# Convolution tiles moved to later heads of a recurrence, and two compressions moved behind the projections around them, in a three-block network on one core

## The chip, the core and the metric

The kernel runs on one core of a Trainium2 chip. The metric is the device time of one execution in microseconds, shown as the median of several runs. TensorE (PE) multiplies matrices, VectorE (DVE) and ScalarE (ACT) do the elementwise work, GpSimd (POOL) has little to do here, and SyncE (SP) issues the loads and stores.

## What is computed

Three blocks run one after the other on 512 tokens of width 1024. The change touches the second and the third.

The second block has an attention branch with compressed keys and values. Of its reference this matters:

```
q, kc, vc, ks, vs, kw, vw, z, gl = jnp.split(h @ w_in_b, ...)
def compress(t, pos, w1, w2):
    blocks = heads_kv(t)[:, :, cmp_idx] + pos
    flat = blocks.reshape(Bsz, N_KV, n_cmp, L_CMP * HEAD_DIM_2)
    return jax.nn.silu(flat @ w1) @ w2
k_cmp = compress(kc, pos_ck, w_ck1, w_ck2)
v_cmp = compress(vc, pos_cv, w_cv1, w_cv2)
...
g = jax.nn.sigmoid(gb)
return g[..., 0:1] * o_cmp + g[..., 1:2] * o_slc + g[..., 2:3] * o_win
```

The third block runs a gated recurrence of eight heads of width 128 in both directions, in chunks of 128 tokens, and beside it a convolution of 31 taps over 1024 channels, which is normalised over the channels:

```
o_lat, _, _ = hgrn2_bidir(pq, pi, pff, pfb, lbs[0, l], lbs[1, l], s_f, s_b)
o = rmsnorm_3(o_hg, gn_w) * silu(heads(g));   y_hg = o.reshape(...) @ w_hg_out
u = cv_a * sigmoid(cv_b)
u = silu(layernorm_3(dwconv1d(u, dw_w, dw_b), ln_w, ln_b));   y_cv = u @ w_cv_out
y = sigmoid(gate_hg) * y_hg + sigmoid(gate_cv) * y_cv
```

The normalisation needs all 1024 channels of the convolution before its first value exists.

## The kernel before

**Products.** A weight tile of 128 x 1024 is loaded (`wr`), split by ScalarE into a rounded part `wh` (L127) and by VectorE into a remainder `wl` (L128), and TensorE multiplies each of the eight pieces three times (L141 to L143). One such product of 24 matmuls is called a form here; it gives 128 output columns for all 512 tokens. Three PSUM buffers hold the forms, so a form can start when the one three before it has been read. The products with 256 columns have lines L182 to L184.

**Order.** The code is written stage by stage, and a scheduler orders the instructions of each engine ahead of time by priority and readiness. Each engine then runs its list strictly in that order and waits where an operand is late.

**Second block.** `blocks` copies the key and value products into strided blocks (L753 on VectorE, L755 on ScalarE). `compress` multiplies them with a loaded matrix (16 matmuls, L765), takes column 124 as a bias (L767), applies SiLU on ScalarE (L770), multiplies again (L775 for keys, L785 for values) and copies the result out (L779, L787). `values(0)` and `values(1)` are forms whose results VectorE copies (L793). The gate logits are one form of 48 columns, copied by ScalarE, transposed by TensorE and passed through Tanh.

**Third block.** The recurrence handles head after head. `gla_gates` makes the decays of two heads (L1009, L1019, L1020), `gla_front` the running sums of a head (L1118 to L1126), and `gla_back` the rest: exponentials and products on six levels (L1144 to L1161, with matmuls L1151 and L1167), masks (L1173 to L1179), the key transposes (L1201), state products (L1206) and the state chain on VectorE (L1209), the output products (L1213 to L1215), the squares (L1219), a reciprocal root in ten small VectorE steps (L225 to L234), the scaling (L1221, one for each head), a transpose (L1226) and the gate (L1227), and the split into `yhgh` and `yhgl` (L132, L133). `gla_back` is emitted at a higher priority.

Beside head j the code emits the pieces that the string `BESIDE[j]` names. `cN` is convolution tile N: two forms, then on VectorE L1260, L1262 and 30 taps L1264 that each update the tile `cy` in place, a store to DRAM, and, some pieces later, the statistics over its transpose (L260 on TensorE, L262 on VectorE). `gN` and `hN` are each one form of gate logits with a Tanh and a store. The string sets the order of emission; the order on the engines is the scheduler's.

After the last head the statistics are closed (L269, the reciprocal root again, and four transposes L253 each for mean and root). Eight forms with `w_hg_out` read all heads (evacuated by L1314); while they run, each channel tile of the convolution is loaded back, reduced by the mean (L1318), scaled (L1319), put through SiLU on ScalarE (L1320) and split (L132, L133, into `ycvh` and `ycvl`). Eight forms with `w_cv_out` then read all of those (evacuated by L1326).

Of the kernel before, what the change touches and what calls it, by code (L numbers as in the profile page):

```python
# [693 lines left out]
def branch_a(k, hT):  # L694

    nc, I = k.nc, k.I
    cw, cb = k.col("conv_w", (P, 8, 3)), k.col("conv_b", (P, 8))
    nc.vector.tensor_scalar(cw, cw, 0.5, None, op0=ALU.mult)
    nc.vector.tensor_scalar(cb, cb, 0.5, None, op0=ALU.mult)
    y = k.b16(F32R, name="yAh"), k.b16(F32R, name="yAl")  # L700
    m = []
    yield y, m
    for j in range(8):
        cg = k.f("cg")
        nc.scalar.activation(cg, k.form_a(I["w_a2"][8 + j], hT), AF.Copy)
        u = k.f("cu", (P, S + 2))
        nc.gpsimd.memset(u[:, :2], 0.0)
        nc.vector.tensor_mul(u[:, 2:], cg, k.form_a(I["w_a2"][16 + j], hT))
        c = k.f("cc")
        nc.vector.tensor_scalar(c, u[:, :S], cw[:, j, 0:1], cb[:, j:j + 1], op0=ALU.mult, op1=ALU.add)  # L710
        nc.vector.scalar_tensor_tensor(c, u[:, 1:S + 1], cw[:, j, 1:2], c, op0=ALU.mult, op1=ALU.add)
        nc.vector.scalar_tensor_tensor(c, u[:, 2:], cw[:, j, 2:3], c, op0=ALU.mult, op1=ALU.add)
        nc.vector.tensor_mul(c, c, k.form_a(I["w_a2"][j], hT))
        z = k.f("cz")
        k.silu2(z, k.form_a(I["w_a2"][24 + j], hT))
        nc.gpsimd.tensor_mul(c, c, z)
        k.split(y[0][:, j], y[1][:, j], c)
        yield
    m.append(k.b16(name="mT"))
    for j in range(8):  # L720
        branch(k, 0, y, hT, m[0], (j,))
        yield


def block2(k, ctx, hT, x2d, x3d):
# [4 lines left out]
    c4 = k.wk.tile([P, 4, P], F32, name="c4", tag="c4", bufs=1)  # L730
# [9 lines left out]
    def blocks(nm):  # L740
        kg = k.b16(shape=(P, 16, 125), name="kg")
        nc.sync.dma_start(out=kg[:, :, 124], in_=I["pos_c" + nm])
        for tl in range(2):
            ps = first.pop(0) if first else k.form_a(I["w_c" + nm][tl], hT)
            for hf in range(2):
                hh = 2 * tl + hf
                v = ps[64 * hf:64 * hf + 64].rearrange("p (j m b) -> p b m j", m=8, b=2)
                for b in range(2):
                    for mh in range(2):
                        o = kg[64 * b:64 * b + 64, 8 * mh:8 * mh + 8, 31 * hh:31 * hh + 31]  # L750
                        i_ = v[:, b, :, mh:mh + 31]
                        if mh:
                            nc.vector.tensor_copy(o, i_)  # L753
                        else:
                            nc.scalar.activation(o, i_, AF.Copy)  # L755
        return kg

    def compress(nm, kg):
        ph = k.mm((P, 125))
        for q in range(2):  # L760
            w1 = k.x4("w1", (P, 8, P))
            nc.sync.dma_start(out=w1, in_=I[f"w_c{nm}1"][:, 8 * q:8 * q + 8])
            for m in range(8):
                mm_i = 8 * q + m
                nc.tensor.matmul(ph, lhsT=w1[:, m], rhs=kg[:, mm_i], start=mm_i == 0, stop=mm_i == 15)  # L765
        pb = k.small((P, 1), "pb", bufs=2)
        nc.vector.tensor_copy(pb, ph[:, 124:125])  # L767
        hs = k.wk.tile([P, 4, 32], F32, name="hs", tag="B", bufs=3)
        nc.vector.memset(hs, 0.0)
        nc.scalar.activation(hs[:, :, :31], ph[:, :124].rearrange("p (h j) -> p h j", h=4), AF.Silu, bias=pb)  # L770
        if nm == "k":
            w2 = k.wk.tile([P, P], F32, name="w2", tag="B", bufs=3)
            nc.sync.dma_start(out=w2, in_=I["w_ck2"])
            pk = k.mm((P, P))
            nc.tensor.matmul(pk, lhsT=w2, rhs=hs.rearrange("p a b -> p (a b)"), start=True, stop=True)  # L775
            pk = pk.rearrange("p (a b j) -> p a b j", a=2, b=2)
            for par in range(2):
                rr = slice(64 * par, 64 * par + 64)
                nc.vector.tensor_copy(kcmp[rr, :, par], pk[rr, :, par])  # L779
        else:  # L780
            w2 = k.wk.tile([P, 64], F32, name="w2", tag="B", bufs=3)
            nc.sync.dma_start(out=w2, in_=I["w_cv2"])
            for kp in range(2):
                pv = k.mm((64, 64))
                nc.tensor.matmul(pv, lhsT=hs[:, 2 * kp:2 * kp + 2].rearrange("p a b -> p (a b)"), rhs=w2, start=True, stop=True)  # L785
                for i in range(2):
                    nc.vector.tensor_copy(vbd[32 * i:32 * i + 32, kp, i], pv[32 * i:32 * i + 32])  # L787
# [3 lines left out]
    def values(b):  # L791
        t = k.x4("vs", (P, NT, 256))
        k.form_b(I["w_vs"][b], hT, lambda i, c, ps: nc.vector.tensor_copy(t[:, i:i + c], ps), nat)  # L793
        VV.append(t)
    first = k.forms_a([I["w_ck"][0], I["w_ck"][1], I["w_cv"][0]], hT)
    kg = blocks("k"), blocks("v")
    values(0)
    compress("k", kg[0])
    values(1)
    compress("v", kg[1])  # L800
    ps = k.form_a(I["w_gl"], hT, n=48)
    gt = k.f("gt", (48, S))
    nc.scalar.activation(gt, ps, AF.Copy)
# [4 lines left out]
    gv = gN.rearrange("p n h b -> p n (h b)")  # L808
    nc.scalar.activation(gv, tps, AF.Tanh, scale=0.5)
    nc.vector.tensor_scalar(gv, gv, 0.5, 0.5, op0=ALU.mult, op1=ALU.add)  # L810
    ON = k.b16(shape=(P, NT, 16, 64), name="ON")
    fill = branch_a(k, hT)
    yA, mA = next(fill)
    lo, hi = slice(0, 64), slice(64, P)
    for kp in range(2):
# [12 lines left out]
        for i in range(4):  # L828
# [31 lines left out]
            for n in range(NT):  # L860
                nc.tensor.matmul(po[:, n].rearrange("p a b -> p (a b)"), lhsT=pt[:, n], rhs=vbd[:, kp].rearrange("p a b -> p (a b)"), start=True, stop=True)
            nc.vector.tensor_mul(ON[:, :, hs], po, l[:, :, :, None].to_broadcast([P, NT, 2, 64]))
            for par in range(2):
# [33 lines left out]
                for b in range(2):  # L897
                    nc.gpsimd.tensor_add(ON[:, :, h], ON[:, :, h], ot[:, :, b])
                next(fill, None)
# [5 lines left out]
    for j in range(8):  # L905
# [3 lines left out]
        for n in range(NT):  # L909
            nc.tensor.transpose(tps[:, n], ON[:, n, 2 * j:2 * j + 2].rearrange("p a b -> p (a b)"), k.ident)  # L910
        c = k.f("cc")
# [67 lines left out]
    v = k.small((P, NT), "rs_v")  # L979
# [116 lines left out]
LEVELS = (128, 64, 32, 16, 8)  # L1096
DIAG = 4
BEFORE = "c0 g0 v0 c1 v1 g1 c2 v2 g2 c3 v3 g3"
BESIDE = ("c4 g4", "c5 g5", "h0 g6", "c6 g7", "h1", "c7 h2", "h3 h4", "h5 h6 h7")


def gla_gates(k, h, hT):
# [128 lines left out]
def block3(k, hT, x3d, out):  # L1231
# [44 lines left out]
    def run(items):  # L1276
        for it in items.split():
            n = int(it[1])
            for t in late:
                t[0] -= 1  # L1280
            while late and late[0][0] < 0:
                late.pop(0)[1]()
            {"c": lambda: conv(n), "v": lambda: value(n), "g": lambda: gate("w_gcv", n, gcd), "h": lambda: gate("w_ghg", n, ghd)}[it[0]]()
# [10 lines left out]
    for j in range(-1, 8):  # L1294
# [7 lines left out]
        with k.tc.high_priority(offset=GLA_AHEAD):  # L1302
            gla_back(k, j, hT, V, R[:, j % 2], q[:, j % 2], tot[j], masks, gnw, DB, y)
        run(BESIDE[j])
    for t in late:
# [99 lines left out]
def body(tc, I, out):  # L1405
    with ExitStack() as es:
        k = K(es, tc, I)
        w = k.w(I["w_in_a"][0], KT, offset=FIRST)
        x = load_x(k)
        k.setup()  # L1410
        x2d = k.dr.tile([P, KT, S], F32, name="x2d")
        x3d = k.dr.tile([P, KT, S], F32, name="x3d")
        k.vec_input(0)
        k.add_vec("Bc", "w_mod", "b_mod", 0)
        k.add_vec("Ac", "w_mod", "b_mod", 1, ("norm1_w",), True)
        k.vec_input(1)
        k.add_vec("B2", "w_ada", "b_ada", 0)
        k.add_vec("A2", "w_ada", "b_ada", 1, ("g_pre",), True)
        k.add_vec("G2", "w_ada", "b_ada", 2, ("g_post",))
        k.vec_input(2)  # L1420
        k.add_vec("B3", "w_mod", "b_mod", 0)
        k.add_vec("A3", "w_mod", "b_mod", 1, ("norm1_w",), True)
        k.add_vec("gt1", "w_mod", "b_mod", 2)
        k.add_vec("B4", "w_mod", "b_mod", 3)
        k.add_vec("A4", "w_mod", "b_mod", 4, ("norm2_w",), True)
        k.add_vec("gt2", "w_mod", "b_mod", 5)
        ctx = ctx_steps(k)
        acc, h1 = block1(k, ctx, w, *x)
        h2 = block1b(k, ctx, acc, h1, x2d)
        h3 = block2(k, ctx, h2, x2d, x3d)  # L1430
        block3(k, h3, x3d, out)
# [128 lines left out]
```

## Time and profile before

| what | value |
|---|---|
| median of 3 runs | 3153.04 us (3151.38 to 3154.02) |
| the profiled execution | 3153.95 us, of which the span is 3152.2 us |
| TensorE busy | 3049.8 us, 97% of the span |
| VectorE busy | 2064.1 us, 65% |
| ScalarE busy | 1255.9 us, 40% |

Shares are means over stages that have different limits. In the recurrence VectorE is busy far above its mean, and in most other stages far below.

### The profile page before, as it was taken

The page shows a single profiled execution, that of the slowest core. Times are in us where ns is not written, and L with a number is a line of the kernel's source. Part 1 is how long each engine was busy: PE and PEld are TensorE (multiplying, and loading weights), DVE is VectorE, ACT ScalarE, POOL GpSimd, SP SyncE. Part 2 cuts the span into 40 slices and gives each one's busy share as a digit, 9 for nine tenths or more (in the row PEclk, how much of TensorE's full clock was granted, in tenths as well). Part 3 has the DMA queues.
Part 4 walks back from the last instruction along what each step waited for, and adds up shares of the span by engine and source line. Part 5 has one row for each costly group of instructions (what it writes and reads, how often), then busy time and mean ns, then how long its engine had stood idle before and what let it go on. Part 6 is the DMA issues. An engine that isn't in the chain of part 4 may idle for free.

```text
span 3152.2 us, 45055 instructions
## 1 busy us (share of the span) xinstructions
PE 3049.8 (97%) x17508; PEld 2538.7 (81%) x17508; DVE 2064.1 (65%) x4223; ACT 1255.9 (40%) x2111; POOL 144.9 (5%) x224
## 2 busy tenths in 40 slices
PE   9999999999999999999999999999998989999998
PEld 7888878787887787778778888889877777888886
DVE  7566665656545745555444364589998996597877
ACT  4333544444442533334443233442454544243322
POOL 0000000000000001110110101000000000100000
PEclk9999999999999999999999999999999999999998
DMA  8324343434322421221122222443222225323332
GB/s 292 101 94 134 103 159 137 159 131 151 129 79 68 135 85 65 67 67 61 54 71 93 94 94 88 139 137 107 94 80 72 88 86 170 107 84 94 96 99 77
DMA packets 113062, 334.43 MB, mean 106 GB/s; under 512 B 17616, under 2 KB 23760, under 8 KB 112848
## 3 DMA queue, kind: packets, MB, share of 16 engines
q1 hardware_dynamic: 112848, 331.54, 31.9%
q8 instruction: 138, 2.26, 0.3%
q14 instruction: 76, 0.62, 0.1%
HBM read 316.82 MB, written 14.68 MB: 105 GB/s over the span
## 4 chain that ended last, share of the span: by engine, by line
PE 47%; DVE 5%; ACT 2%; issue 1%; DVEq 0%; ACTq 0%
PE mm L141 13%; PE mm L142 13%; PE mm L143 13%; PE O L891 1%; PE mm L182 1%; PE mm L183 1%; PE mm L184 1%; DVE wl L128 1%; PE S L875 1%; PE T L884 1%; ACT wh L127 0%; PE S L1167 0%; DVE cy L1264 0%; PE S L1206 0%; PE S L942 0%
## 5 line engine op out<-in xcount | busy, mean ns | idle before, releaser
L127 ACT ACTIVATE wh<-wr 128x1024 fp32r<-128x1024 f32 (+2 forms) x499 | 503.2, 1010 | 1084.0 <-PE mm L142 799.6
L128 DVE TENSOR_TENSOR wl<-wr,wh 128x1024 fp32r<-128x1024 f32 (+2 forms) x499 | 605.1, 1214 | 426.2 <-ACT wh L127 422.1
L141 PE MATMUL mm<-h2h,wh 128*128 128x512 f32 (+1 forms) x752 | 300.8, 400 | 7.7 <-DVE kg L753 6.8
L142 PE MATMUL mm<-h2l,wh 128*128 128x512 f32 (+1 forms) x752 | 300.3, 399 | 0.0
L143 PE MATMUL mm<-h2h,wl 128*128 128x512 f32 (+1 forms) x752 | 300.2, 399 | 0.0
L141 PE MATMUL mm<-h3h,wh 128*128 128x512 f32 x488 | 193.8, 403 | 7.7 <-ACT th L1270 4.2
L142 PE MATMUL mm<-h1l,wh 128*128 128x512 f32 x488 | 198.8, 407 | 0.0
L141 PE MATMUL mm<-h1h,wh 128*128 128x512 f32 x488 | 197.5, 405 | 0.0
L143 PE MATMUL mm<-h1h,wl 128*128 128x512 f32 x488 | 197.2, 404 | 0.0
L142 PE MATMUL mm<-h3l,wh 128*128 128x512 f32 x488 | 193.5, 401 | 0.0
L143 PE MATMUL mm<-h3h,wl 128*128 128x512 f32 x488 | 193.2, 401 | 0.0
L1264 DVE SCALAR_TENSOR_TENSOR cy<-uc,dww,cy 128x512 f32<-128x512 f32 x240 | 176.9, 746 | 2.4
L141 PEld LDWEIGHTS mm<-h2h,wh 128*128 128x128 f32 (+1 forms) x752 | 141.7, 188 | 34.2 <-issue 7.2
L142 PEld LDWEIGHTS mm<-h2l,wh 128*128 128x128 f32 (+1 forms) x752 | 141.8, 189 | 25.2
L143 PEld LDWEIGHTS mm<-h2h,wl 128*128 128x128 f32 (+1 forms) x752 | 141.5, 188 | 24.6
L369 DVE CUSTOM_DVE_ANT_0 gr<-gr,crow 128x256 f32<-128x256 f32 x352 | 131.5, 425 | 42.9 <-DMA gr<-in_w_mod 31.4
L141 PE MATMUL mm<-h4h,wh 128*128 128x512 f32 (+1 forms) x368 | 140.5, 382 | 0.0
L143 PE MATMUL mm<-h4h,wl 128*128 128x512 f32 (+1 forms) x368 | 140.5, 382 | 0.0
L142 PE MATMUL mm<-h4l,wh 128*128 128x512 f32 (+1 forms) x368 | 140.5, 382 | 0.0
L1369 DVE SCALAR_TENSOR_TENSOR fc<-up,fdw,fc 128x512 f32<-128x512 f32 x176 | 132.2, 751 | 5.1
L881 ACT ACTIVATE pe<-sb,nm 128x128 f32<-128x128 f32 (+3 forms) x128 | 71.4, 558 | 119.4 <-DVE nm L878 119.2
L141 PEld LDWEIGHTS mm<-h3h,wh 128*128 128x128 f32 x488 | 93.2, 191 | 27.8 <-ACT th L1270 4.7
(532 smaller groups left out, 7238.5 us busy)
## 6 DMA issues: line engine op xcount, KB each, us to landing
gr<-in_w_mod SPq DMA_DIRECT2D x64, 512.0 KB, 5.1
wr<-in_w_up SPq DMA_DIRECT2D x44, 512.0 KB, 3.5
wr<-in_w_in_a SPq DMA_DIRECT2D x32, 512.0 KB, 3.5
wr<-in_w_f SPq DMA_DIRECT2D x32, 512.0 KB, 3.5
wr<-in_w_v SPq DMA_DIRECT2D x32, 512.0 KB, 3.8
wr<-in_w_in_b SPq DMA_DIRECT2D x32, 512.0 KB, 3.5
wr<-in_w_a SPq DMA_DIRECT2D x32, 512.0 KB, 3.5
gr<-in_w_ada SPq DMA_DIRECT2D x24, 512.0 KB, 4.5
```

The lines of the kernel that those rows point to most:

```text
L127: self.nc.scalar.activation(h, r, AF.Copy)
L128: self.nc.vector.tensor_sub(l, r, h.bitcast(F32))
L141: mm(ps, lhsT=wh[:, k], rhs=xh[:, k0 + k, tok], start=first and k == 0, stop=False)
L142: mm(ps, lhsT=wh[:, k], rhs=xl[:, k0 + k, tok], start=False, stop=False)
L143: mm(ps, lhsT=wl[:, k], rhs=xh[:, k0 + k, tok], start=False, stop=last and k == kt - 1)
L182: mm(ps, lhsT=sel(xh, k), rhs=wh[:, kk], start=st, stop=False)
L183: mm(ps, lhsT=sel(xh, k), rhs=wl[:, kk], start=False, stop=False)
L184: mm(ps, lhsT=sel(xl, k), rhs=wh[:, kk], start=False, stop=en)
L369: nc.vector.tensor_tensor_reduce(out=r[:, sl], in0=r[:, sl], in1=self.crow[:, sl], scale=1.0, scalar=0.0, op0=ALU.mult, op1=ALU.add, accum ...
L881: nc.scalar.activation(pe, sb, AF.Exp, bias=m, scale=-1.0, accum_out=lt[:, n, b:b + 1])
L1264: nc.vector.scalar_tensor_tensor(c, u[:, t:t + S], dww[:, j, t:t + 1], c, op0=ALU.mult, op1=ALU.add)
L1369: nc.vector.scalar_tensor_tensor(c, u[:, a:a + 8, b:b + 64], fw[:, j, t:t + 1], c, op0=ALU.mult, op1=ALU.add)
```

## The change

Two independent pieces of order are edited. In the second block both compressions are emitted after the second `values` and after the gate logits; before, one compression stood behind each `values`. In the third block the string `BESIDE` deals the last four convolution tiles and the gates to the heads in another order: tiles 4, 5, 6 and 7 stood beside heads 0, 1, 3 and 5 and now stand beside heads 0, 3, 6 and 7. No instruction is added to or taken from the work itself.

```diff
     first = k.forms_a([I["w_ck"][0], I["w_ck"][1], I["w_cv"][0]], hT)
     kg = blocks("k"), blocks("v")
     values(0)
-    compress("k", kg[0])
     values(1)
-    compress("v", kg[1])
     ps = k.form_a(I["w_gl"], hT, n=48)
     gt = k.f("gt", (48, S))
     nc.scalar.activation(gt, ps, AF.Copy)
@@
     nc.scalar.activation(gv, tps, AF.Tanh, scale=0.5)
     nc.vector.tensor_scalar(gv, gv, 0.5, 0.5, op0=ALU.mult, op1=ALU.add)
+    compress("k", kg[0])
+    compress("v", kg[1])
     ON = k.b16(shape=(P, NT, 16, 64), name="ON")
@@
-BESIDE = ("c4 g4", "c5 g5", "h0 g6", "c6 g7", "h1", "c7 h2", "h3 h4", "h5 h6 h7")
+BESIDE = ("c4 h0 g4", "h1 g5", "h2", "c5 h3 g6", "h4 g7", "h5", "c6 h6", "h7 c7")
```

**First place: TensorE at the compressions.** Before, the key compression stands between the two `values` products (L182 to L184, from which two rows are shown on either side):

```order
L183 MATMUL mm<-wl,h2h 128x256
L184 MATMUL mm<-wh,h2l 128x256
L765 MATMUL mm<-kg,w_9609 128x125 x8
L765 MATMUL mm<-kg,w_9619 128x125 x8
L775 MATMUL mm<-hs,w_9634 128x128
L182 MATMUL mm<-wh,h2h 128x256
L183 MATMUL mm<-wl,h2h 128x256
```

Of the changed kernel, from the last matmuls of the gate logits on:

```order
L142 MATMUL mm<-h2l,wh 48x512
L143 MATMUL mm<-h2h,wl 48x512
L765 MATMUL mm<-kg,w_9763 128x125 x7
L804 MATMUL T<-ident,gt 128x48 x4
L765 MATMUL mm<-kg,w_9763 128x125
L765 MATMUL mm<-kg,w_9773 128x125 x8
L775 MATMUL mm<-hs,w_9788 128x128
L765 MATMUL mm<-kg,w_9795 128x125 x8
L765 MATMUL mm<-kg,w_9805 128x125 x8
L785 MATMUL mm<-w_9820,hs 64x64 x2
```

Both compressions now stand in one piece behind the gate logits, whose transposes (L804) have moved in among the key compression's matmuls; the key and the value compression have only each other to cover their waits.

**Second place: VectorE in the middle of the recurrence, at the mask steps and the state chain of head 2** (L1177, L1179 and L1209; the taps of a convolution tile are L1264). Before, at the second mask step:

```order
L1177 COPY_PREDICATED D<-masks,S 128x128
L1264 SCALAR_TENSOR_TENSOR cy<-uc,dww,cy 128x512
L128 TENSOR_TENSOR wl<-wr,wh 128x1024
L1264 SCALAR_TENSOR_TENSOR cy<-uc,dww,cy 128x512
L1179 COPY_PREDICATED A<-masks,D 128x512
L1264 SCALAR_TENSOR_TENSOR cy<-uc,dww,cy 128x512
L262 BN_STATS bst<-T 128x6
```

The same steps of the changed kernel:

```order
L1177 COPY_PREDICATED D<-masks,S 128x128
L1209 SCALAR_TENSOR_TENSOR SS<-SS,dec,S 128x128
L1179 COPY_PREDICATED A<-masks,D 128x512
L1209 SCALAR_TENSOR_TENSOR SS<-SS,dec,S 128x128 x2
L1118 SCALAR_TENSOR_TENSOR R_18837<-rst,sp 128x512
```

Before, a tap stood behind nearly every step of head 2, its state chain included; now the masks and the state chain follow one another and no tap stands there.

**Third place: VectorE behind the last head.** Before, the closing root (L223 is its last step) stands ahead of the first evacuation of a `w_hg_out` form (L1314):

```order
L223 SCALAR_TENSOR_TENSOR rs_y<-rs_t,rs_y 128x4
L128 TENSOR_TENSOR wl<-wr,wh 128x1024
L233 TENSOR_TENSOR rs_a<-rs_y 128x4
L234 TENSOR_TENSOR rs_a<-rs_a,rs_c 128x4
L223 SCALAR_TENSOR_TENSOR rs_y<-rs_a,rs_y 128x4
L1314 SCALAR_TENSOR_TENSOR yT<-th,mm 128x512
L1318 TENSOR_TENSOR cy<-cy,S 128x512
```

Of the changed kernel, from the seventh of the eight evacuations on:

```order
L1314 SCALAR_TENSOR_TENSOR yT<-th,mm 128x512
L128 TENSOR_TENSOR wl<-wr,wh 128x1024
L1264 SCALAR_TENSOR_TENSOR cy<-uc,dww,cy 128x512 x6
L128 TENSOR_TENSOR wl<-wr,wh 128x1024
L262 BN_STATS bst<-T 128x6 x2
L269 BN_AGGR mv_22772<-bst 128x2 x2
```

The taps of tile 7 and the closing statistics now stand beside the `w_hg_out` forms, and the normalisation (L1318, L1319) stands behind the last of the eight evacuations; before, it stood among them.

## Rows read from the trace of the kernel before

**Rows 1.** The page, part 1: busy time and share of each engine.
```profile
PE 3049.8 (97%) x17508; PEld 2538.7 (81%) x17508; DVE 2064.1 (65%) x4223; ACT 1255.9 (40%) x2111; POOL 144.9 (5%) x224
```

**Rows 2.** The waits of PE over the run: total us, times, longest.
```profile
PE mm L301 <- DVE ss L294: 13.2, 4, 5.3
PE O L1215 <- DVE SS L1209: 9.9, 2, 7.4
PE mm L141 <- DVE kg L753: 6.8, 1, 6.8
...
PE S L1151 <- DVE rs_y L226: 4.6, 1, 4.6
```

**Rows 3.** Windows between the eight L1221: busy us and instructions, clock, DMA.
```profile
core 0: us, PE busy (x) PEld busy (x) DVE busy (x) ACT busy (x) POOL busy (x), PEclk, DMA share, GB/s
...
2289.05:2354.03 64.98, 57.85 (x533) 46.16 (x531) 63.76 (x111) 33.54 (x45) 0.16 (x2) 0.95 0.26 86
2354.03:2400.74 46.71, 37.06 (x290) 29.57 (x289) 44.71 (x88) 18.56 (x42) 0.16 (x2) 0.89 0.18 63
2400.74:2452.83 52.09, 50.61 (x510) 40.48 (x508) 44.53 (x82) 31.98 (x42) 0.00 (x0) 1.00 0.22 74
2452.83:2506.58 53.75, 51.18 (x431) 41.17 (x427) 53.01 (x95) 22.85 (x40) 0.16 (x2) 1.00 0.26 87
2506.58:2545.63 39.05, 38.72 (x432) 30.50 (x424) 38.27 (x74) 29.39 (x46) 0.00 (x0) 1.00 0.24 74
2545.63:2595.04 49.41, 44.69 (x303) 36.00 (x298) 48.05 (x85) 20.64 (x38) 0.00 (x0) 0.97 0.29 92
2595.04:2622.32 27.28, 19.84 (x291) 16.66 (x292) 21.23 (x54) 14.12 (x31) 3.85 (x6) 0.75 0.15 48
2622.32:2672.60 50.28, 50.07 (x229) 41.20 (x228) 34.55 (x61) 22.16 (x28) 0.00 (x0) 1.00 0.72 226
```

**Rows 4.** Windows, a stretch of the first block that holds only forms.
```profile
100.00:150.00 50.00, 50.00 (x222) 41.44 (x221) 20.69 (x24) 13.61 (x17) 0.23 (x2) 1.00 0.34 113
```

**Rows 5.** VectorE's groups by form, 2289 to 2622 us: first and last of 41.
```profile
L1264 DVE SCALAR_TENSOR_TENSOR cy<-uc,dww,cy 128x512 f32<-128x512 f32 x116 | 86.3, 744 | 0.0
L128 DVE TENSOR_TENSOR wl<-wr,wh 128x1024 fp32r<-128x1024 f32 x41 | 50.1, 1221 | 4.0 <-ACT wh L127 3.5
...
L1119 DVE MEMSET R<- 128x1 f32 x5 | 0.3, 59 | 0.0
```

**Rows 6.** VectorE's timeline: start us, us; runs of one line.
```profile
2226.07 3.90 DVE L1264 SCALAR_TENSOR_TENSOR cy<-uc,dww,cy 128x512 f32<-128x512 f32 x5
...
2587.65 1.89 DVE L1158 TENSOR_TENSOR E<-R 128x512 f32<-128x512 f32 x3
```

**Rows 7.** TensorE's timeline at the two compressions.
```profile
1103.49 3.73 PE L765 MATMUL mm<-kg,w 128*128 128x125 f32 x32
1109.51 0.49 PE L775 MATMUL mm<-hs,w 128*128 128x128 f32 x2 [2.28 <-ACT hs L770]
1121.34 3.73 PE L765 MATMUL mm<-kg,w 128*128 128x125 f32 x32
1125.79 0.45 PE L785 MATMUL mm<-w,hs 128*64 128x64 f32 x4 [0.71 <-ACT hs L770]
```

**Rows 8.** ScalarE's timeline there and at the SiLU of the normalisation.
```profile
1107.79 1.28 ACT L770 ACT_TABLE_LOAD   x1 [3.53 <-DVE pb L767]
1109.09 0.36 ACT L770 ACTIVATE hs<-mm,pb 128x124 f32<-128x124 f32 x1
...
1132.72 0.58 ACT L803 ACTIVATE gt<-mm 48x512 f32<-48x512 f32 x1
...
2637.90 1.28 ACT L1320 ACT_TABLE_LOAD   x1 [3.22 <-DVE cy L1319]
2639.20 0.82 ACT L1320 ACTIVATE cy<-cy,clb,clw 128x512 f32<-128x512 f32 x1
2639.92 1.04 ACT L127 ACTIVATE wh<-wr 128x1024 fp32r<-128x1024 f32 x1
2640.87 0.61 ACT L132 ACTIVATE ycvh<-cy 128x512 fp32r<-128x512 f32 x1
```

**Rows 9.** TensorE's timeline after its wait for the block copies L753.
```profile
1084.94 0.76 PE L141 MATMUL mm<-h2h,wh 128*128 128x512 f32 x1 [6.81 <-DVE kg L753]
...
1088.07 0.42 PE L142 MATMUL mm<-h2l,wh 128*128 128x512 f32 x1
```

**Rows 10.** VectorE's timeline behind the last head: the last split and the last evacuation.
```profile
2658.36 0.69 DVE L133 TENSOR_TENSOR ycvl<-cy,ycvh 128x512 fp32r<-128x512 f32 x1
...
2671.93 0.69 DVE L1314 SCALAR_TENSOR_TENSOR yT<-th,mm 128x512 f32<-128x512 f32 x1 [3.35 <-PE mm L143]
```

## The prediction, made before the changed kernel was run

> **What bounds the kernel now.** I read the page first. TensorE is busy for 97% of the span and VectorE for 65% [rows 1], so over the whole run only TensorE's gaps can be won back, about 100 us of them. The list of what TensorE waited for comes next [rows 2]: its largest entries sit in the final stage and at the block copies, which the change does not touch, but the state chain of the recurrence (L1209) holds it for 9.9 us in two waits and another VectorE step for 4.6 us in one. The third view cuts the recurrence at the eight scalings L1221 [rows 3]. I call the piece that ends at head k's scaling stretch k. The reader should compare three columns. In stretches 1, 2, 4 and 6 VectorE is busy for 63.8 of 65.0, 44.7 of 46.7, 53.0 of 53.7 and 48.1 of 49.4 us, so VectorE ends those stretches, and TensorE idles for 7.1, 9.7, 2.6 and 4.7 us in them. In stretches 3 and 5 TensorE is nearly full. In stretch 7 neither is: TensorE works for 19.8 of 27.3 us, because the list ahead of the last scaling has little but the head's own chain. Together the seven take 333.3 us with 33.3 us of TensorE idle. The piece behind head 7, up to the first `w_cv_out` matmul, is TensorE alone: 50.1 of 50.3 us, with VectorE at 34.6.
>
> So this is a stage in which two engines take turns as the bound, and what an edit of the order can win is TensorE's idle time, at most the 33 us, less whatever it opens elsewhere.
>
> **The change part by part: the recurrence.** I counted the form matmuls in TensorE's order per stretch. Before they are 194, 110, 168, 183, 121, 152 and 37; after, 211, 63, 177, 162, 192, 70 and 132. The sum rises from 965 to 1007, because forms that used to follow (a gate, tile 7, and the first 28 matmuls of `w_hg_out`) now run ahead of head 7's scaling. One takes 0.225 us (222 in 50 us, [rows 4]). What a stretch of before takes beyond its forms is 21.3, 22.0, 14.3, 12.6, 11.8, 15.2 and 19.0 us [rows 3]: the head's own small matmuls and the idle time. The four stretches 3 to 6 have a mean of 13.5, with 11.8 and 15.2 as ends.
>
> For VectorE I took every instruction of the order at the mean of its group [rows 5], less 0.08 us, since consecutive ones overlap by that much (three of 0.684 us take 1.89, [rows 6]). For before this gives 63.6, 44.4, 44.1, 53.1, 38.1, 47.8 and 20.3 us, within 1 us of the busy column, so the count can be trusted. For after it gives 66.6, 19.3, 44.7, 45.1, 51.6, 24.7 and 37.1. The reason is the taps L1264: 26, 30, 0, 30, 0, 27 and 3 before; 26, 0, 0, 29, 1, 0 and 25 after, and 35 of them (5 of tile 6, all 30 of tile 7) behind head 7.
>
> Now each stretch of after has a limit that I can name. Stretch 1 stays VectorE's: 66.6 plus the 1.2 us that VectorE idled there before, 67.8. Stretch 2 loses all its taps, and I walked its chain: the state products reach VectorE at about 9 us, the last L1209 ends near 15, the output products near 18, the squares and the root near 22, while TensorE has 63 forms (14.2 us) and about 10 us of small matmuls, so 24.2. Stretch 6 walks the same way to 27.0, ended by TensorE again. For stretches 3, 4, 5 and 7 TensorE's list is longer than VectorE's, so I take forms plus 13.5: (177 + 162 + 192 + 132) x 0.225 + 4 x 13.5 = 203.2. The sum is 322.2 against 333.3: **-11.1 us**. The ends: all six TensorE stretches (796 forms, 179.1 us) with 11.8 beside them give 317.7 (-15.6), with 15.2 they give 338.1 (+4.8).
>
> **Behind head 7.** Before, the first `w_cv_out` matmul comes 50.3 us after the last scaling, and the normalised tiles are all ready 13 us before that: the last split starts at 2658.36, the last evacuation at 2671.93 [rows 10]. So the normalisation was hidden. After, TensorE has 164 `w_hg_out` matmuls left, 36.9 us, and is done about 38.9 us behind the scaling. VectorE meanwhile has 35 taps, nine weight splits, seven evacuations and a few more. Taps in a row cost more than taps between other work: five take 3.90 us [rows 6], 0.79 us each after the first, against 0.67 when another instruction stands between. Twenty of the 35 follow one another, so they take 25.9 us, the splits 10, the rest 7; the last tap ends near 43, the closing statistics near 47. Then come the subtraction, the scaling, the SiLU with its table load of 1.28 us [rows 8], and the split: the first `w_cv_out` matmul starts near 51.5, 12.6 us after TensorE ran dry. From there VectorE delivers a tile every 1.9 us. The order interleaves the first `w_cv_out` forms by tile, so TensorE can follow, and I find the first 50 matmuls done near 64.4. Before, 50 matmuls are done at 50.3 + 11.3 = 61.6. That is +2.8.
>
> TensorE will also come back at the lower clock. After the 6.81 us wait at the block copies the granted clock is 0.69 in the window that follows; seven matmuls then take 3.13 us instead of 1.58 [rows 9], so such a return costs 1.5 us. With it the piece is **+4 us**; it could be +1 if the taps interleave better, and +10 if VectorE also waits at each evacuation.
>
> **The compressions.** TensorE executes the same 64 small passes, 3.73 us for each compression, and the waits of 2.28 and 0.71 us for the SiLU [rows 7] stay, since behind L775 there is still nothing ready that the order puts first except the value compression, which comes after it. New is that the four transposes of the gate logits stand among the key matmuls: the logits' copy on ScalarE (0.58 us, [rows 8]) now stands behind a weight split and is waited for, about 0.3 us, and the Tanh needs a table of its own ahead of the SiLU. I take **+0.6 us**; the ends are 0 (all covered) and +4 (the SiLU waits for both table loads and the weights `w2`, whose load now stands behind two loads of `w_a` in SP's list).
>
> On that table the page "ScalarE: Activation LUTs" of the Trainium skill, section "What ACT_TABLE_LOAD costs", says that a switch takes about 1.28 us of loading and about 1.38 us more of draining. This trace shows the first part alone: the SiLU starts 0.02 us after the load ends, at both places of [rows 8]. By the page each of the two exposed switches would cost 1.4 us more, and the sum below would lose 2.8 us of its gain; that is a rival, with the smallest chance.
>
> **Sum.** +0.6 - 11.1 + 4 = -6.5 us on the profiled 3153.95 us, 3147.4. That execution lies 0.9 us above the median, so on the median it is **3146.5 us**.
>
> **Rivals.** (a) *The gain is given back behind head 7.* If VectorE waits at the evacuations as well, that piece costs +10, and the sum is -0.5: 3152.5. For it speaks that both engines are then within a few us of each other; against it, that three PSUM buffers let TensorE run ahead. (b) *More gain.* The stretches reach 11.8 us beside their forms and the end costs +1: -15.6 + 1 + 0.6 gives 3139. Stretch 5 shows that 11.8 is possible [rows 3]. (c) *Slower.* The changed order mixes head chains of two engines with fewer taps to fill VectorE, so TensorE waits at more hand-offs. If what stands beside the forms is 15.2 in each of the six, as in stretch 6 of before, the recurrence takes 338.1 and the sum is +9.4: 3162. From 14.7 on it decides (slower by 6.3). Against it stands that stretch 6 of before ended on VectorE, which the new stretches do not. (d) *The table drain of the page*: -6.5 + 2.8 gives 3149.
>
> **How the numbers follow.** A measurement of this kernel can tell about 0.2%, 6.3 us, from no change. The forecast with its neighbours (3142 to 3150) gets 0.43, (a) 0.22, (b) 0.18, (c) 0.13, (d) 0.04. Of the forecast's share I put 0.26 below 3146.7. So faster by over 0.2%: 0.44; within it: 0.43; slower: 0.13. The range takes (b) at its value and reaches half way into (c): 3137 to 3157.
>
> **What would show it.** In the trace of after: stretches 2 and 6 near 24 and 27 us with VectorE no longer full; the seven together near 322; head 7's scaling 11 us earlier; then a gap of TensorE of 10 to 13 us between the last `w_hg_out` and the first `w_cv_out` matmul, named as a wait for the root or for the split, and a granted clock below 1 there; the 35 taps behind head 7. At the compressions, waits at L775 and L785 as before and a short one at the transposes L804. I would be wrong if stretches 2 and 6 stay above 35 us (then the chain's own latency, not the taps, set them), if the gap behind `w_hg_out` is under 3 us or over 20, or if the stall moves to a place that I did not walk: the start of the recurrence, or the loads behind the store of tile 7 in SP's list.

## The result, and the profile after

The changed kernel takes 3134.68 us (median of 4 runs, 3133.19 to 3137.35), the kernel before 3153.11 us beside it: a ratio of 0.9945 (95% interval 0.9933 to 0.9958), 18.4 us faster. The forecast was 6.6 us faster, and the lower end of its range was 3137. The sign was right, the gain nearly three times as large.

Page, part 1, of the changed kernel, against [rows 1]:

```profile
PE 3045.6 (97%) x17508; PEld 2532.9 (81%) x17508; DVE 2061.2 (66%) x4223; ACT 1257.0 (40%) x2112; POOL 147.8 (5%) x224
```

The span went from 3152.2 to 3133.6 us, 18.6 us. TensorE's busy time fell by 4.2 us, so its idle time fell by 14.4, from 102.4 to 88.0 us. The waits of TensorE over the run, against [rows 2] (total us, times, longest):

```profile
PE mm L301 <- DVE ss L294: 12.9, 4, 5.0
PE mm L141 <- DVE kg L753: 6.8, 1, 6.8
...
PE S L253 <- DVE rs_y L223: 4.3, 4, 1.8
PE O L1215 <- DVE SS L1209: 3.3, 1, 3.3
PE mm L141 <- ACT ycvh L132: 2.9, 1, 2.9
```

The wait for the state chain L1209 has gone from 9.9 to 3.3 us, and that of 4.6 us for a root is gone. Behind the last head waits have grown: the one for the closing root (L223) from 0.2 to 1.8 us (the other waits of that line stand in both kernels), and the one for the first split of the normalised tiles (`ycvh`) is new. Where the time came from is read in the windows between the scalings, against [rows 3], with the same columns; the last two rows are the piece behind head 7 up to the first `w_cv_out` matmul, and its end from the last `w_hg_out` matmul on:

```profile
2286.62:2355.51 68.89, 62.60 (x545) 49.95 (x545) 67.19 (x114) 35.50 (x47) 0.00 (x0) 0.95 0.27 87
2355.51:2379.41 23.90, 23.90 (x258) 19.76 (x254) 20.23 (x52) 15.08 (x39) 0.00 (x0) 1.00 0.18 56
2379.41:2432.81 53.40, 51.39 (x513) 40.97 (x511) 45.19 (x83) 31.25 (x43) 0.16 (x2) 1.00 0.27 85
2432.81:2478.97 46.16, 45.81 (x346) 36.94 (x342) 45.04 (x81) 20.83 (x39) 0.00 (x0) 1.00 0.28 95
2478.97:2537.05 58.08, 55.90 (x589) 44.51 (x590) 52.04 (x93) 39.51 (x57) 0.16 (x2) 1.00 0.28 90
2537.05:2561.95 24.90, 24.90 (x266) 20.11 (x265) 24.50 (x58) 14.54 (x31) 0.30 (x1) 1.00 0.24 73
2561.95:2601.02 39.07, 37.66 (x307) 30.39 (x306) 37.68 (x73) 16.41 (x34) 3.70 (x8) 1.00 0.37 114
...
2601.02:2651.03 50.01, 42.42 (x189) 33.59 (x187) 48.67 (x84) 12.39 (x14) 0.00 (x0) 0.92 0.51 161
2639.90:2651.03 11.13, 3.54 (x15) 1.86 (x13) 10.81 (x30) 4.43 (x6) 0.00 (x0) 0.63 0.41 132
```

The seven stretches take 314.4 us where they took 333.3, and TensorE idles for 12.2 us in them instead of 33.3. Outside the first stretch nothing is left of the granted clocks of 0.89, 0.97 and 0.75. Behind the last scaling lie 532.6 us (529.9 before), and ahead of the first 2.4 us less. That is -18.9 + 2.7 - 2.4 = -18.6.

The last window of [rows 3] ends a little late for this comparison. TensorE's timeline of the kernel before has its first `w_cv_out` matmul here:

```profile
2671.73 0.39 PE L141 MATMUL mm<-ycvh,wh 128*128 128x512 f32 x1
```

That is 49.4 us behind the last scaling; the window's end at 2672.60, 50.3 us behind it, lies 0.9 us late. So of the +2.7 us the changed kernel loses 0.6 up to that matmul (50.0 against 49.4) and 2.1 behind it.

The end of the piece behind head 7, in TensorE's timeline (start us, us, the wait in brackets):

```profile
2639.90 0.39 PE L143 MATMUL mm<-yhgh,wl 128*128 128x512 f32 x1
2642.01 0.63 PE L260 MATMUL T<-ident,cy 128*128 128x128 f32 x4 [1.72 <-DVE cy L1264]
2643.73 1.55 PE L253 MATMUL S<-ident,mv 128*128 128x128 f32 x4 [1.09 <-DVE mv L269]
2647.06 1.12 PE L253 MATMUL S<-ident,rs_y 128*128 128x128 f32 x4 [1.78 <-DVE rs_y L223]
2651.03 1.22 PE L141 MATMUL mm<-ycvh,wh 128*128 128x512 f32 x2 [2.85 <-ACT ycvh L132]
2653.15 0.80 PE L142 MATMUL mm<-ycvl,wh 128*128 128x512 f32 x1 [0.90 <-DVE ycvl L133]
```

TensorE is dry at 2640.3 and reads the first normalised tile at 2651.0: 10.7 us in which only small transposes run, at a granted clock of 0.63. Each of them names VectorE's last tap, the statistics or the root as what it waited for.

TensorE at the compressions, against [rows 7]:

```profile
1117.41 1.72 PE L765 MATMUL mm<-kg,w 128*128 128x125 f32 x14
1119.10 0.45 PE L804 MATMUL T<-ident,gt 48*128 48x48 f32 x4
1119.48 2.27 PE L765 MATMUL mm<-kg,w 128*128 128x125 f32 x18
1123.74 0.71 PE L775 MATMUL mm<-hs,w 128*128 128x128 f32 x2 [1.98 <-ACT hs L770]
1124.24 5.18 PE L765 MATMUL mm<-kg,w 128*128 128x125 f32 x32
1130.13 0.45 PE L785 MATMUL mm<-w,hs 128*64 128x64 f32 x4 [0.71 <-ACT hs L770]
```

ScalarE there, against [rows 8]:

```profile
1122.03 1.28 ACT L770 ACT_TABLE_LOAD   x1 [0.77 <-DVE pb L767]
1123.32 0.36 ACT L770 ACTIVATE hs<-mm,pb 128x124 f32<-128x124 f32 x1
```

The waits at L775 and L785 are those of before (1.98 and 0.71 us against 2.28 and 0.71), and the transposes L804 do not wait. ScalarE has one instruction more than before (2112), a second table load: one for the Tanh, one for the SiLU behind it. But the value compression takes 5.18 us, where it took 3.73. Its stretch in the changed kernel and in the kernel before:

```profile
1123.74:1130.60 6.86, 6.15 (x39) 5.90 (x39) 0.87 (x5) 0.36 (x1) 0.00 (x0) 0.75 0.03 7
1121.34:1126.30 4.96, 4.25 (x39) 4.00 (x38) 3.17 (x5) 1.42 (x2) 0.00 (x0) 1.00 0.44 142
```

Behind TensorE's wait for the SiLU the granted clock is 0.75 on average (1.00 before): fourteen of the 32 records come 0.21 us apart, at the lower of the two clock levels, and the others 0.11. Of the nine traces with the compressions moved, six show this (5.1 to 5.4 us) and three do not (3.73); the three traces with the compressions in their old place do not. The prediction had 3.73 us for each.

### The profile page after: what moved, and what is told of

Its sections match the earlier page's. It is cut to its first block, busy times and chain, and to the rows that moved or that the text cites. A ratio compares the mean times of both kernels' runs of the same rounds, so it can differ in the third digit from the quotient of the medians.

```text
span 3133.6 us, 45064 instructions
## 1 busy us (share of the span) xinstructions
PE 3045.6 (97%) x17508; PEld 2532.9 (81%) x17508; DVE 2061.2 (66%) x4223; ACT 1257.0 (40%) x2112; POOL 147.8 (5%) x224
## 4 chain that ended last, share of the span: by engine, by line
PE 46%; DVE 6%; ACT 1%; issue 1%; DVEq 0%; ACTq 0%
PE mm L142 13%; PE mm L141 13%; PE mm L143 13%; PE O L891 1%; DVE wl L128 1%; PE mm L182 1%; PE mm L183 1%; PE mm L184 1%; PE S L875 1%; PE T L884 1%; DVE cy L1264 0%; PE S L1167 0%; ACT wh L127 0%; PE S L1206 0%; PE S L942 0%
## 5 line engine op out<-in xcount | busy, mean ns | idle before, releaser
L1264 DVE SCALAR_TENSOR_TENSOR cy<-uc,dww,cy 128x512 f32<-128x512 f32 x240 | 176.9, 748 | 3.4
L143 PEld LDWEIGHTS mm<-h2h,wl 128*128 128x128 f32 (+1 forms) x752 | 141.7, 188 | 24.9
L624 ACT ACTIVATE pe<-sb,ml 128x256 f32<-128x256 f32 (+1 forms) x128 | 63.1, 493 | 118.5 <-DVE ml L622 117.8
```

The lines of the kernel that those rows point to most:

```text
L143: mm(ps, lhsT=wl[:, k], rhs=xh[:, k0 + k, tok], start=False, stop=last and k == kt - 1)
L624: nc.scalar.activation(pe[:, a, c0:], sb[:, a, c0:], AF.Exp, bias=m, scale=-1.0, accum_out=ml[g][:, n, 2 + hh:3 + hh])
L1264: nc.vector.scalar_tensor_tensor(c, u[:, t:t + S], dww[:, j, t:t + 1], c, op0=ALU.mult, op1=ALU.add)
```

## The experiments

Two theories of the recurrence were put against each other. **Theory S**: a stretch lasts as long as the longer of the two engines' own lists (VectorE's instructions, or TensorE's forms and small products), and the change won by moving taps out of stretches in which VectorE's list was the longer one. **Theory F**: TensorE idled for want of forms ahead of the last scalings, and the change won by the gates that it moved. Both list sums were counted in each kernel's order. The first expectations (e3, e4) price TensorE's small products too low: they give the changed kernel 343.9 us for the eight pieces, which took 364.4. From e5 on the prices are fitted to the changed kernel's stretches, so that its own agreement is no test.

| run | edit | median us | before beside it | ratio (95%) |
|---|---|---|---|---|
| e1 | compressions only | 3152.73 | 3152.27 | 1.0000 (0.9991 to 1.0009) |
| e2 | `BESIDE` only | 3134.93 | 3152.27 | 0.9944 (0.9931 to 0.9956) |
| e3 | tiles moved, gates not | 3144.58 | 3152.27 | 0.9973 (0.9963 to 0.9983) |
| e4 | gates moved, tiles not | 3152.99 | 3152.27 | 1.0002 (0.9993 to 1.0011) |
| e5 | before, 120 taps left out | 3110.49 | 3151.75 | 0.9871 (0.9856 to 0.9886) |
| e6 | changed, 120 taps left out | 3111.55 | 3151.75 | 0.9872 (0.9858 to 0.9885) |
| e7 | changed, 20 taps of tile 7 left out | 3123.24 | 3151.75 | 0.9913 (0.9899 to 0.9927) |
| e8 | new deal | 3146.90 | 3151.75 | 0.9987 (0.9978 to 0.9996) |
| e9 | e8 with tile 6 one head earlier | 3130.67 | 3151.82 | 0.9932 (0.9919 to 0.9944) |
| e10 | a deal with even lists | 3132.97 | 3151.82 | 0.9941 (0.9928 to 0.9955) |

**e1 and e2: each half alone.** e1 is the changed kernel with the old `BESIDE`, e2 the kernel before with the new one.

> Only the compressions are moved; BESIDE is that of the kernel before. Theory 1 (the whole gain comes from BESIDE): 3153 to 3156 us, no gain, +2 at most, as TensorE's waits at L775 and L785 are the same in both traces. Theory 2 (part of the gain lies ahead of the recurrence, where the trace of after has the first scaling L1221 2.4 us earlier and the first matmul behind the block copies 4.3 us earlier): 3149 to 3151 us.

> Only BESIDE is changed; the compressions stand as in the kernel before. Theory 1: 3133 to 3136 us, the whole 18.4 us. Theory 2: 3137 to 3139 us, and the first scaling L1221 at 2289 us as before.

The whole gain is `BESIDE`'s: e2 has 17.3 us of it, e1 none. The 2.4 us ahead of the first scaling are scatter between executions. In e1's trace that scaling starts at 2285.01, 4 us earlier than in the kernel before, and its median is no faster. In e2 the value compression, ahead of which nothing was changed, starts at 1119.41, where the kernel before has 1121.34. Over the eight experiments with all taps or all but 20 of tile 7's the first scaling lies between 2284.25 and 2288.91. A cost of 1.5 us, such as the lower clock at the value compression, is below what e1's interval (2.8 us either way) can tell.

**e3 and e4: the two halves of the string.** The edits to the changed kernel are

```diff
-BESIDE = ("c4 h0 g4", "h1 g5", "h2", "c5 h3 g6", "h4 g7", "h5", "c6 h6", "h7 c7")
+BESIDE = ("c4 g4", "g5", "h0 g6", "c5 g7", "h1", "h2", "c6 h3 h4", "h5 h6 h7 c7")   # e3
+BESIDE = ("c4 h0 g4", "c5 h1 g5", "h2", "c6 h3 g6", "h4 g7", "c7 h5", "h6", "h7")   # e4
```

> The compressions as changed; the convolution tiles stand beside heads 0, 3, 6 and 7 as in the changed kernel, but the gates beside the heads of the kernel before. By the order TensorE has only 918 form matmuls ahead of head 7's scaling (965 before, 1007 changed) and 250 behind it; the taps are 26, 0, 0, 30, 0, 0, 30 and 30 behind head 7. Theory S (each piece lasts as long as the engine with the longer list, VectorE or TensorE, whichever that is, and spreading the taps is what won): the larger lists sum to 354.5 us against 364.2 before and 343.9 changed, so about 10 us faster than before, 3143 us; no gap behind w_hg_out. Theory F (TensorE's idle time is a want of forms ahead of the last scalings, and the place of the taps does not matter): slower than before, 3153 to 3163 us, as 47 form matmuls fewer stand there.

> The compressions as changed; the gates stand beside the heads of the changed kernel, but the convolution tiles beside heads 0, 1, 3 and 5 as in the kernel before. By the order TensorE has 1009 form matmuls ahead of head 7's scaling (1007 changed), and the taps are 26, 30, 0, 30, 0, 25, 5 and none behind head 7. Theory S: the larger lists sum to 359.5 us against 364.2 before, so about 5 us faster than before, 3148 us, with VectorE full in stretches 2, 4 and 6. Theory F: as fast as the changed kernel or faster, since the forms are there and nothing is late behind head 7: 3125 to 3136 us.

Windows of e3, the seven stretches and the piece behind head 7:

```profile
2288.91:2597.18 308.27, 283.25 (x2710) 226.27 (x2709) 290.01 (x544) 167.99 (x281) 4.32 (x12) 0.98 0.26 81
...
2597.18:2659.40 62.22, 62.15 (x280) 50.63 (x279) 49.38 (x82) 16.66 (x19) 0.00 (x0) 0.99 0.49 156
```

The same of e4:

```profile
2288.08:2632.76 344.68, 313.25 (x2809) 251.19 (x2808) 316.61 (x585) 172.79 (x286) 4.32 (x12) 0.94 0.25 80
2632.76:2672.90 40.14, 39.99 (x183) 32.40 (x182) 32.33 (x59) 19.60 (x25) 0.00 (x0) 1.00 0.75 238
```

TensorE's longest wait in the seventh stretch of e4, from its timeline:

```profile
2611.41 1.08 PE L1151 MATMUL S<-QD,KD 128*32 128x32 f32 x64 [10.16 <-ACT KD L1146]
```

Tiles alone win 7.7 us; gates alone win nothing, although they put 1009 form matmuls ahead of the last scaling, as the changed kernel does. Theory F falls. Theory S holds for e3 (3143 forecast) and misses e4 by 5 us (3148 forecast). And the halves are not additive, 7.7 and -0.7 against 17.3. Tiles alone shorten the recurrence by 25 us (308.3 against 333.3) and give 13 back behind head 7, where 250 form matmuls are left over (62.2 us against 49.4); another 3 us are lost behind the first `w_cv_out` matmul, where VectorE still normalises (483.9 us to the end of the span against 480.5). Gates alone take these forms away from the end (40.1 us) and put them into stretches that VectorE ends anyway, and in stretch 7 they are missing: 27 form matmuls, and a wait of 10.2 us, which the sum of lists did not contain. Together the gates fill the stretches that the taps have left.

**e5 and e6: no taps at all.** In both kernels the taps of tiles 4 to 7 are left out; what they would add to the convolution is missing.

```diff
-        for t in range(1, 31):
+        for t in range(1, 31 if j < 4 else 1):
```

> The kernel before, with the 30 taps of each of the convolution tiles 4 to 7 left out (120 VectorE instructions, some 80 us); forms, stores and statistics stay, and the scheduler orders anew. Theory S (the taps in the wrong stretches made VectorE the longer list): TensorE's list is now the longer one in all eight pieces, 355 us in all against 374 with the taps, so about 3125 to 3130 us, and TensorE's idle time in the recurrence falls below 10 us. Theory F (the forms are in the wrong stretches): nothing much is won, 3145 us or more.

> The changed kernel with the same 120 taps left out. Theory S: TensorE's lists sum to 355 us here too, so within 4 us of the kernel before without taps, 3122 to 3130 us: without the taps the deal of BESIDE is worth nothing. Theory F: the 17 us between the two kernels stay, 3120 us or less against 3137 or more.

The seven stretches of e5 in one window:

```profile
2280.91:2568.16 287.25, 281.95 (x2735) 227.34 (x2734) 236.57 (x464) 167.92 (x282) 4.38 (x12) 1.00 0.27 86
```

And those of e6:

```profile
2279.74:2572.23 292.49, 287.24 (x2754) 230.86 (x2753) 236.96 (x460) 172.11 (x286) 4.29 (x12) 1.00 0.27 88
```

Without the taps the two deals differ by 1.1 us, within the scatter: the deal was worth its 17 us only because of the taps. TensorE idles for 5.3 us in each recurrence, where it idled for 33.3 and 12.2. Both came out 10 us or more below the expectation. TensorE's fitted lists (355 us for the eight pieces) were too long by 7 to 9 us (346 and 348 measured). The first scaling also came 7 to 8 us earlier than with the taps (2280.9 and 2279.7); four taps of tile 4 that stood ahead of it explain some 3 us, and the rest is not explained here.

**e7: the price of the late normalisation.** The loop stops at `11` for tile 7, so 20 taps are left out.

> The changed kernel with 20 of the 30 taps of tile 7 left out, so that 15 taps stand behind head 7 and not 35. What the late normalisation costs (a stall of 10.7 us, the return at the lower clock and a first product paced by VectorE): if it is all given back, the first w_cv_out matmul comes 41 us behind the last scaling instead of 50.0, with a granted clock of 1.00, and the time is 3122 to 3125 us. If the stall only hides another wait (the loads of the convolution tiles behind the store of tile 7, or w_cv_out's weights), 3130 us or more.

Its piece behind head 7, up to the first `w_cv_out` matmul:

```profile
2601.33:2642.20 40.87, 40.84 (x189) 32.95 (x188) 39.73 (x75) 17.12 (x22) 0.00 (x0) 1.00 0.62 199
```

The stall is gone, the clock stays at 1.00, and from the last scaling to the end of the span this kernel takes 521.1 us where the changed one takes 532.6, 11.5 us less. So the taps behind head 7 cost all of that, and no load stood behind them. It showed as +2.7 us alone, because the same change had taken some 9 us of forms out of this piece (164 form matmuls instead of 203).

**e8, e9 and e10: can the lists be evened out further?** Deals that make both lists alike in every stretch, on top of the changed kernel:

```diff
+BESIDE = ("c4 g4 h0 g5", "h1", "h2", "h3 c5", "h4 g6", "h5 h6", "g7 c6 c7", "h7")   # e8
+BESIDE = ("c4 g4 h0 g5", "h1", "h2", "h3 c5", "h4 g6", "c6 h5 h6", "g7 c7", "h7")   # e9
+BESIDE = ("c4 g4 h0 g5", "h1", "h2", "h3 c5", "g6", "h4 c6 h5", "h6 g7 c7", "h7")   # e10
```

> Another deal on top of the changed kernel, found by adding up both engines' lists in every piece: tile 5 behind gate h3, tile 7 beside head 6 behind tile 6, gates 5 and h6 one head earlier, g7 two later. Nothing is left out. The taps per stretch are 26, 0, 0, 23, 7, 0, 41 and 19 behind head 7, so that both lists are within 3 us of one another in every stretch. Theory S: the larger lists sum to 354 us, where the changed kernel has 363 and 4 us of late normalisation: 3120 to 3124 us, no stall behind w_hg_out. If chains between the engines set the time once the lists are even: no better than the changed kernel, 3133 to 3140 us.

e8 missed its expectation by some 25 us. About 20 are in stretch 7, and behind the last head TensorE waits once for 6.7 us for an evacuation (L1314), since VectorE still has 19 taps there. Its windows of stretches 5, 6 and 7:

```profile
2471.21:2524.50 53.29, 53.06 (x569) 42.20 (x570) 53.04 (x93) 36.25 (x48) 0.00 (x0) 1.00 0.25 85
2524.50:2549.66 25.16, 25.16 (x268) 19.20 (x257) 25.13 (x57) 16.20 (x34) 0.32 (x4) 1.00 0.28 87
2549.66:2620.35 70.69, 67.72 (x378) 47.07 (x378) 50.89 (x94) 17.60 (x34) 3.83 (x6) 0.98 0.25 80
```

Both lists of stretch 7 were counted at 50 to 51 us, and VectorE is busy for 50.9, but TensorE is busy for 67.7 of 70.7 with only 3.0 us idle. Its timeline there:

```profile
2578.86 0.25 PE L1167 MATMUL S<-E 128*32 128x32 f32 x2
2579.03 0.51 PE L141 MATMUL mm<-h3h,wh 128*128 128x512 f32 x1
2579.47 0.25 PE L1167 MATMUL S<-E 128*32 128x32 f32 x2
2579.65 0.50 PE L142 MATMUL mm<-h3l,wh 128*128 128x512 f32 x1
2580.08 0.25 PE L1167 MATMUL S<-E 128*32 128x32 f32 x2
2580.26 0.49 PE L143 MATMUL mm<-h3h,wl 128*128 128x512 f32 x1
```

A place of the changed kernel's timeline where the same small products stand together:

```profile
2499.66 0.46 PE L1167 MATMUL S<-E 128*32 128x32 f32 x32
2500.05 0.50 PE L142 MATMUL mm<-h3l,wh 128*128 128x512 f32 x1
```

In e8 a form matmul and one small product (two records) repeat every 0.61 us. Apart, the form matmul takes 0.225 and the product 0.39 / 16 = 0.024 us. Each turn so costs some 0.36 us more, and TensorE's order has 40 of them in stretch 7, 15 in stretch 6 and at most 8 in the others (by time, between the scalings, the trace has 45 and 9). The 40 make 14.4 of the 16.9 us by which TensorE is busy beyond its list. The next two runs were chosen to tell this from a theory of chains.

> The deal of e8 with one edit: tile 6 stands beside head 5 and no longer beside head 6. In e8 TensorE's order in stretch 7 changed 40 times from a form matmul to a pair of the small level products L1167, and there a form matmul and a pair took 0.61 us together (0.225 and 0.03 apart, by the stretches of the changed kernel); here it changes 5 times in stretch 6 and twice in stretch 7. Theory S with a price for the mixing (0.33 us for each change beyond 7): the larger lists sum to 355 us where the changed kernel has 367, so 3121 to 3126 us, and a stretch 7 near 26 us. If the chains between the engines were what held e8 back: 3135 us or more again.

> A deal with both engines' lists within 3 us of one another in stretches 1 to 7 except the third, at most 8 changes from forms to small products in each, and 14 taps behind head 7. Nothing is left out. Theory S with the price for mixing: the larger lists sum to 353 us (318 ahead of the last scaling, 36 behind it with no stall), 3119 to 3124 us, faster than the changed kernel by 0.3 to 0.5%. If the chains set the time once the lists are even: 3133 us or more.

The one edit of e9 wins back 16.2 us. Its stretches 5, 6 and 7:

```profile
2471.92:2520.80 48.88, 48.47 (x486) 38.91 (x485) 48.52 (x88) 32.16 (x44) 0.16 (x2) 1.00 0.27 86
2520.80:2579.39 58.59, 55.17 (x501) 44.74 (x499) 57.68 (x102) 26.62 (x44) 0.81 (x3) 0.99 0.28 94
2579.39:2609.69 30.30, 27.39 (x229) 21.56 (x218) 26.44 (x59) 11.40 (x28) 3.24 (x5) 0.84 0.28 88
```

The edit moves forms and taps too, so the median alone would not name the cause. TensorE's busy time does: over the three stretches it falls from 145.9 to 131.0 us, with more forms in them and not fewer, while its idle time grows from 3.2 to 6.7 us. So the mixing, and not waiting on chains, made the three stretches of e8 long (149.1 us against 137.8). Behind the last head e9 gains another 6 us (39.8 against 46.0), where the wait of 6.7 us is gone. But neither e9 nor e10 reached 3119 to 3126: their eight pieces take 361.8 and 362.6 us where the lists sum to 355 and 353. Where the two lists are equal, hand-offs of 1 to 4 us that nothing covers show again. e9 and the changed kernel both beat the kernel before; their intervals overlap, and which of them is faster stays open.

## Why the prediction was wrong, point by point

| term | forecast | measured | what the runs say |
|---|---|---|---|
| compressions | +0.6 (0 to +4) | no change (e1) | waits as forecast, none at L804; a lower clock not forecast |
| stretch 1 | 67.8 | 68.9 | VectorE's list, as forecast |
| stretch 2 | 24.2 | 23.9 | TensorE's, as forecast |
| stretch 6 | 27.0 | 24.9 | TensorE's, no idle time |
| stretches 3, 4, 5, 7 | 203.2 | 196.7 | 53.4, 46.2, 58.1 and 39.1 |
| seven stretches | -11.1 (-15.6 to +4.8) | -18.9 | 7.8 us too small |
| behind head 7 | +4 (+1 to +10) | +2.7 | stall of 10.7 us, forecast 12.6 |

**The step that failed** is the term for stretches 3, 4, 5 and 7, "forms plus 13.5". The 13.5 us were the mean of what stretches 3 to 6 of before took beside their forms. But the prediction had just read that VectorE ended stretches 4 and 6 of before; what stood beside the forms there held 2.6 and 4.7 us of TensorE's idle time [rows 3]. The term carried that wait into stretches in which, by the prediction's own count, VectorE's list was no longer the longer one (stretch 4 kept 29 of its taps, and VectorE still did not end it). What is beside the forms was 13.6, 9.7, 14.9 and 9.4 us, 6.5 us less in all than the term has. Idle time is about half of that: 9.1 us in stretches 3 to 6 of before, 6.0 in stretches 3, 4, 5 and 7 of after. The other half is busy time: fewer small products, and in stretch 6 of before a granted clock of 0.97. Stretches 4 and 7 missed the term by 3.8 and 4.1 us: TensorE idles there for 0.35 and 1.4 us, and none of the products L1151 stand in them (128 records in each of stretches 3 and 5). The low end, 11.8 us from the one stretch without idle time, came from a stretch with more small products than stretches 4 and 7 (192 records of L1167 against 128, and 64 of L1151), which fits a low end of 317.7 us where 314.4 were measured. VectorE's list had been counted instruction by instruction; TensorE's small products had not, and a constant stood for them. The 2.1 us of stretch 6 are a mis-sized chain.

The rest of the miss is small: 1.3 us of the end, and ahead of the first scaling 0.6 forecast for the compressions and 2.4 of scatter in the profiled execution. Two more readings of the prediction were off. With the window's late end the prediction put 50 `w_cv_out` matmuls of before done at 61.6 us behind the last scaling, where the trace has 60.9; after, they are done at 64.7. And the range was said to take (b) at its value, which is 3139, but was put at 3137; the measured time lies below both.

**What was right.** The scalings as cuts, VectorE's counted lists (19.3 and 24.7 us forecast for stretches 2 and 6, 20.2 and 24.5 busy), stretches 2 and 6 as TensorE's, and most of the chain behind head 7: TensorE dry 38.9 us after the scaling (39.3 measured), the last tap near 43 (40.8), the first `w_cv_out` matmul near 51.5 (50.0), with a granted clock below 1. One link was not there: the SiLU's table load, which the forecast put behind the scaling, ran at 2641.17, while the first SiLU starts at 2648.94, so it cost nothing. e7 shows that the stall is the taps' and costs 11 us.

**The rivals.** (a), the gain given back behind head 7 by waits at the evacuations, did not come: the piece cost +2.7, and neither engine waits at an evacuation there (in e8 TensorE does, for 6.7 us). (b), more gain, was the nearest, but it stopped at the 11.8 us beside the forms. (c), slower by hand-offs, did not come. (d), the drain that the page "ScalarE: Activation LUTs" of the Trainium skill adds to a table switch (section "What ACT_TABLE_LOAD costs"), is not there in this trace either: the SiLU starts 0.01 us after its load of 1.28 us ends, and e1 shows no cost of the moved compressions beyond its scatter.

Open is how the 17.3 us of e2 divide between idle time and clock. TensorE's busy time fell by 4.2 us with the same work, and granted clocks of 0.75 to 0.97 are gone from three stretches; that the clock made those 4.2 us was not tried by itself.

## What to carry to other kernels

Where two engines take turns as the bound, count the own list of both, small instructions too, and take the longer one stretch by stretch; the remainder of a stretch that another engine ended contains the wait for that engine and must not be carried to one in which it no longer ends. Filler work is worth something only where the other engine leaves room for it, so two halves of a deal can each be worth little and together much. The longer list is a floor: even lists bring back hand-offs of some us, and the order within TensorE's list has a price too.

## What the runs showed of the hardware

**Turns between large and small products.** A form matmul (128 x 128 weights) and a small product L1167 (128 x 32) in turns take 0.61 us a pair in e8, against 0.25 us when each kind stands together. The page "TensorEngine Tiling (Array Packing)" of the Trainium skill says, under "Key Properties", that a change of the tiling mode drains TensorE. The trace agrees in that each turn costs some 0.36 us. The two kinds also differ in their number formats: the forms read operands written as fp32r, the small products plain f32. But by the kernel's code the output products L1213 read plain f32 too, with 128 x 128 weights, and e8 has one of them alone between forms:

```profile
2447.32 0.39 PE L141 MATMUL mm<-h3h,wh 128*128 128x512 f32 x1
2447.55 0.38 PE L1213 MATMUL O<-V,A 128*128 128x128 f32 x2
2447.69 0.47 PE L142 MATMUL mm<-h3l,wh 128*128 128x512 f32 x1
2448.00 0.39 PE L143 MATMUL mm<-h3h,wl 128*128 128x512 f32 x1
```

From the first form matmul to the third are 0.68 us. Two form matmuls at 0.225 us and the product's two records, 0.11 us each where such products stand together, make 0.67. So the change of format alone costs nothing to speak of there, and the price goes with the small shape. No run tried the small products in the other format.

**Busy is not at work.** In e8's seventh stretch TensorE is busy for 96% at a granted clock of 0.98 and does the work of some 50 us in 70.7. Neither the list of waits nor the clock shows it; the pitch of the matmuls does.
